# Output stage of a hybrid decoder layer: residual rows of x in the four tiles of the RWKV bonus terms instead of the ring of eleven

## The chip, the cores and the metric

The kernel runs on one core of a Trainium2 chip. A core has a matrix engine (TensorE, here PE), a vector engine (VectorE, DVE), a scalar engine (ScalarE, ACT), a general engine (GpSimd, POOL) and a sync engine (SyncE, SP); each works through its own list of instructions in order, and they wait for each other by semaphores. Tiles live in SBUF, matmul results in eight PSUM banks. Data moves by DMA, which SP and ACT issue here. The metric is the time of one execution on the device in microseconds (us), as the median of several runs.

## The reference

One layer over 2048 tokens of width 1024, in float32. Three branches read the normalised x: RWKV-7 time mixing (a), sliding-window attention with a window of 128 (b), and cross-attention into 256 memory tokens (c). Each branch is projected, weighted by a sigmoid gate and summed; one more projection and the residual end the layer.

```python
h = rms_norm(x, norm_g[l])
p = h @ w_in[l]
...
bonus = jnp.sum(rh * kh * r_k.astype(f32), axis=-1, keepdims=True) * vh
return y + bonus.reshape(bsz, t, RW_WIDTH)
...
merged = (gates[:, :, 0] * (y_a @ w_proj_a[l]) + gates[:, :, 1] * (y_b @ w_proj_b[l])
          + gates[:, :, 2] * (y_c @ w_proj_c[l]))
x = x + (merged.astype(x.dtype) @ w_out[l]).astype(x.dtype)
```

The bonus term of the second fragment and the last line are what the change touches.

## The kernel before

**Blocks and stages.** The tokens are worked in four blocks of 512 (`sb` 0 to 3). In a block come the projections with RWKV, attention and cross-attention woven together; then the gates and projections of branch a (`merge`, with gates from `gate`), which finish the eight merged sums; then `output`. Ahead of `output`, the block also prepares the next one: `rope_tables` (L554 to L587) makes the rotary tables from `positions`; `x_scales` loads the next 512 rows of x in eight pieces (L1326, on ACT's queue), squares and sums them on ACT (L1328), adds the halves on DVE (L1330), turns the sums into scales, and spreads them over a tile with a copy (L543) and transposes on PE (L545); `x_cols` loads x transposed (L1344), multiplies by the scales (L1347) and splits the result in two (L1350).

**Matmuls in three.** Every number that goes through a large matmul is split into a high part, rounded on ACT, and a remainder, on DVE; each product then takes three matmuls (high by high, high by low, low by high). For a block of weights, `wblock` loads into a tile `raw` (L486 issues on SP), splits on ACT (L487) and DVE (L488) into a tile `whl`, and, in block 0, stores `whl` to memory (L491), so that blocks 1 to 3 load it ready (L483). The projection of L505 to L507 is the general matmul of this kind. `split_y` splits a finished branch (L1032 ACT, L1033 DVE), `split_acc` the merged sums (L1289 ACT, L1291 DVE).

**The output stage** (`output`, L1294 to L1309) makes the 1024 columns in two halves `n`. A half has four PSUM banks, one for each 128 tokens, `mm`, `as_`, `mm`, `as_`, two tiles of each name, so the second half takes the same four banks as the first. Eight weight blocks follow each other, and each is multiplied into the four banks (L1301 to L1303: 8 x 4 x 3 matmuls a half). Then for each of the four banks a tile is taken, a 128x512 piece of x is loaded into it on ACT's queue (L1307), DVE adds half the bank to it in place (L1308; the merged sums carry a factor of two), which frees the bank, and the tile is written out, on ACT's queue too (L1309).

**Tiles.** Tiles of one name share a fixed number of buffers, given out in turn, first in, first out; a request waits until the buffer that is next has been let go. The row tile of `output` is a `g2`, of which there are eleven (`NG`). `g2` also holds the gates of branch a (L1269), the high parts of the merged sums (`a` in L1288, one for each of the eight k, all read until the last matmul of the second half), and other gates earlier in the block. The tiles named `ya` (pool `yp`, four buffers) hold the RWKV bonus term of each of four pairs of heads: written at L839 while the block's RWKV inputs are prepared, added to and gated at L1009 and L1010, and last read by the split of branch a (L1032, L1033), ahead of the merge. The name also serves for the first four tiles of x transposed at the start of the program.

**What sets the order.** The code is not run in the order in which it is written. A planner (`steps`, `lay_out`, `order`) takes all instructions with their dependences, models each engine's clock with a duration for each instruction, and hands every engine its list: among those that can start it takes the lowest rank, which is roughly the place in the program, with weight loads and splits up to 1000 places ahead and the reads of PSUM up to 600. An instruction that is the first to use a tile is offered only when the tile's turn has come and a buffer is free in the model. A change of tiles therefore changes the lists. The DMAs of SP and ACT take eight semaphores in turn (`DMAHW0` to `DMAHW7` below), across both queues; a DMA that comes to a semaphore waits, on the engine that issues it, until the DMA before it on that semaphore has landed.

Of the kernel before, what the change touches and what calls it, by code (L numbers as in the profile page):

```python
# [316 lines left out]
def build(tc, A, nsb=4):  # L317
# [19 lines left out]
    def g2(dt=F32, shape=(128, TB)):  # L337
        return gp_.tile(list(shape), dt, name="g2")
# [3 lines left out]
    def mm_ps():  # L342
        return ps.tile([128, 512], F32, name="mm", bufs=2)
# [4 lines left out]
    def s_ps():  # L348
        return ps.tile([128, 512], F32, name="as_", bufs=2)
# [40 lines left out]
    def yrow(name):  # L390
        return yp.tile([128, TB], F32, name=name)
# [88 lines left out]
    def wblock(src, key=None):  # L480
        w = wp.tile([128, 2, 512], F32R, name="whl")
        if key in kept:
            nc.sync.dma_start(w.bitcast(F32), kept[key])  # L483
            return w[:, 0], w[:, 1]
        raw = wp.tile([128, 512], F32, name="raw", bufs=RAW)
        nc.sync.dma_start(raw, src)  # L486
        S.activation(w[:, 0], raw, AF.Copy)  # L487
        V.tensor_tensor(w[:, 1], raw, w[:, 0].bitcast(F32), op=ALU.subtract)  # L488
        if key is not None and nsb > 1:
            kept[key] = dp.tile([128, 2, 512], F32, name=f"k{len(kept)}")  # L490
            nc.sync.dma_start(kept[key], w.bitcast(F32))  # L491
        return w[:, 0], w[:, 1]
# [801 lines left out]
    def output(sb, mh, ml):  # L1294
        for n in range(2):
            op = [mm_ps(), s_ps(), mm_ps(), s_ps()]
            for k in range(8):
                wh, wl = wblock(A["w_out"][n, k], ("out", n, k))
                for tt in range(4):
                    tk = slice(tt * 128, (tt + 1) * 128)  # L1300
                    PE.matmul(op[tt], mh[k][:, tk], wh, start=k == 0, stop=False)  # L1301
                    PE.matmul(op[tt], mh[k][:, tk], wl, start=False, stop=False)  # L1302
                    PE.matmul(op[tt], ml[k][:, tk], wh, start=False, stop=k == 7)  # L1303
            for tt in range(4):
                rows = slice(sb * TB + tt * 128, sb * TB + (tt + 1) * 128)
                xr = g2()
                nc.scalar.dma_start(xr, A["x"][rows, n * 512:(n + 1) * 512])  # L1307
                V.scalar_tensor_tensor(xr, op[tt], 0.5, xr, op0=ALU.mult, op1=ALU.add)  # L1308
                nc.scalar.dma_start(A["out"][rows, n * 512:(n + 1) * 512], xr)  # L1309
# [53 lines left out]
    for sb in range(nsb):  # L1363
# [9 lines left out]
        ya, yb, yc_ = ([], []), ([], []), ([], [])  # L1373
# [45 lines left out]
        if rb is not None:  # L1419
            hT = x_cols(sb + 1, rb)  # L1420
        output(sb, *zip(*parts))
    order(tc, manual, groups, follow)
    es.close()
# [90 lines left out]
```

## Time and profile before

| | |
|---|---|
| median of 3 timed runs | 2163.45 us (2163.43 to 2164.69) |
| the profiled execution | 2162.26 us, of which the span of the profile is 2160.5 |
| PE | 99% of the span busy, 14260 matmuls |
| DVE | 1556.2 us busy, 72% |
| ACT | 830.3 us busy, 38% |
| POOL | 131.9 us busy, 6% |
| DMA | 511.87 MB, 237 GB/s over the span |

A row of a group of instructions reads: line, engine, operation, out<-in by the names of the program with their shapes, how many; busy time, the mean of one in ns; the idle time of the engine just before them, and what ended it. A list of waits gives the engine and the waiting line, who ended the wait, and us in total, how often, and the longest. A timeline row gives the start in us, the duration, and in brackets the wait ahead of it. The table of windows gives for a stretch from A to B its length, the busy time of each of PE, DVE, ACT, POOL and SP (with the count of instructions that were alone in it in brackets), then the granted TensorE clock as a share of full speed, the busy share of the DMA engines, and GB/s.

### The profile page before, as it was taken

How to read it: one execution, taken by the hardware profiler on the slowest of the kernel's cores; microseconds unless marked ns; L12 is line 12 of the kernel's file. 1: busy time of each engine (PE TensorE's matmuls, PEld its weight loads, DVE VectorE, ACT ScalarE, POOL GpSimd, SP SyncE). 2: the span in 40 equal slices, each digit the busy share in tenths (PEclk: the TensorE clock that was granted, in tenths of full speed). 3: DMA queues.
4: the chain of work that ended last, by engine and by line, in shares of the span. 5: the costliest groups of instructions: out<-in, count | busy, mean ns of one | idle time of the engine just before them, and what ended most of it. 6: DMA issues, size and time to landing. Idle time of an engine off the chain costs nothing.

```text
span 2160.5 us, 37816 instructions
## 1 busy us (share of the span) xinstructions
PE 2132.1 (99%) x14260; PEld 1757.0 (81%) x14260; DVE 1556.2 (72%) x3731; ACT 830.3 (38%) x1757; POOL 131.9 (6%) x159
## 2 busy tenths in 40 slices
PE   8999999999999999999999999999999999999999
PEld 6888787777788888878888888887888888887887
DVE  7799999567578979754627988955455798894532
ACT  6655554336244353303414344421522434431220
POOL 2001000001000000001000100000100000000100
PEclk9999999999999999999999999999999999999999
DMA  9988787978866566585876656676676655758556
GB/s 324 333 273 266 256 280 236 345 272 307 322 231 206 181 211 203 182 293 179 279 260 208 197 185 205 207 250 212 230 259 233 208 184 194 225 173 288 184 193 204
DMA packets 254758, 511.87 MB, mean 237 GB/s; under 512 B 38256, under 2 KB 120432, under 8 KB 254576
## 3 DMA queue, kind: packets, MB, share of 16 engines
q1 hardware_dynamic: 238448, 480.08, 66.8%
q10 hardware_dynamic: 16128, 29.37, 4.1%
q8 instruction: 113, 1.85, 0.3%
q14 instruction: 69, 0.57, 0.1%
HBM read 375.67 MB, written 133.69 MB: 236 GB/s over the span
## 4 chain that ended last, share of the span: by engine, by line
PE 82%; DVE 8%; DMA 6%; issue 1%; ACT 1%; SPq 0%; POOL 0%; ACTq 0%; DVEq 0%; POOLq 0%
PE mm L507 20%; PE mm L505 20%; PE mm L506 20%; DVE whl L488 2%; DMA rt<-in_x 1%; DMA k<-whl 1%; PE mm L1303 1%; PE mm L1301 1%; PE mm L1302 1%; PE rw L983 1%; PE rw L966 1%; PE oo L1250 1%; PE rw L806 1%; DVE ibc L863 1%; PE rw L826 1%
## 5 line engine op out<-in xcount | busy, mean ns | idle before, releaser
L505 PE MATMUL mm<-hH,whl 128*128 128x512 f32 x1888 | 746.0, 395 | 2.9 <-DVE carry L714 2.8
L506 PE MATMUL mm<-hL,whl 128*128 128x512 f32 x1888 | 743.5, 394 | 1.5 <-DVE hL L1350 1.4
L507 PE MATMUL mm<-hH,whl 128*128 128x512 f32 x1888 | 744.6, 394 | 0.0
L505 PEld LDWEIGHTS mm<-hH,whl 128*128 128x128 f32 x1888 | 355.1, 188 | 74.4 <-ACT g L1018 3.2
L506 PEld LDWEIGHTS mm<-hL,whl 128*128 128x128 f32 x1888 | 355.4, 188 | 72.2 <-DVE hL L1350 2.5
L507 PEld LDWEIGHTS mm<-hH,whl 128*128 128x128 f32 x1888 | 355.3, 188 | 70.9
L487 ACT ACTIVATE whl<-raw 128x512 fp32r<-128x512 f32 x162 | 101.6, 629 | 155.7 <-PE mm L507 105.2
L505 PE MATMUL mm<-yh,whl 128*128 128x512 f32 x384 | 151.0, 394 | 2.8 <-ACT ibc L1328 1.6
L507 PE MATMUL mm<-yh,whl 128*128 128x512 f32 x384 | 151.9, 395 | 0.0
L506 PE MATMUL mm<-yl,whl 128*128 128x512 f32 x384 | 150.7, 392 | 0.0
L488 DVE TENSOR_TENSOR whl<-raw,whl 128x512 fp32r<-128x512 f32 x162 | 111.6, 690 | 41.6 <-ACT whl L487 39.7
L863 DVE STREAM_SHUFFLE ibc<-Nc 128x496 f32<-128x496 f32 (+30 forms) x248 | 114.2, 472 | 0.0
L1269 ACT ACTIVATE gt<-mm 128x512 f32<-128x512 f32 x64 | 38.0, 594 | 190.0 <-PE mm L507 189.8
L864 DVE TENSOR_TENSOR ibc<-ibc,Yi 128x496 f32<-128x496 f32 (+30 forms) x248 | 104.5, 421 | 4.2
L865 DVE TENSOR_TENSOR Yi<-Yi,ibc 128x496 f32<-128x496 f32 (+30 forms) x248 | 103.3, 417 | 1.0
L505 PEld LDWEIGHTS mm<-yh,whl 128*128 128x128 f32 x384 | 72.1, 188 | 18.5 <-ACT ibc L1328 2.0
L506 PEld LDWEIGHTS mm<-yl,whl 128*128 128x128 f32 x384 | 72.2, 188 | 15.3 <-DVE yl L1033 0.4
L507 PEld LDWEIGHTS mm<-yh,whl 128*128 128x128 f32 x384 | 72.1, 188 | 15.3
L463 POOL TENSOR_SCALAR st<-st 128x4 f32<-128x4 f32 (+1 forms) x32 | 13.1, 409 | 1031.5 <-DVE st L1060 468.9
L1308 DVE SCALAR_TENSOR_TENSOR g<-mm,g 128x512 f32<-128x512 f32 x16 | 11.0, 690 | 88.5 <-PE mm L1303 88.5
L1284 DVE SCALAR_TENSOR_TENSOR gt<-gt,mm 128x512 f32<-128x512 f32 x32 | 22.0, 686 | 68.5 <-PE mm L507 68.1
L1218 ACT ACTIVATE g<-g,mxs,st 128x128 f32<-128x128 f32 x128 | 61.5, 484 | 18.7 <-DVE mxs L1211 18.7
(1836 smaller groups left out, 3678.5 us busy)
## 6 DMA issues: line engine op xcount, KB each, us to landing
whl<-k SPq DMA_DIRECT2D x486, 512.0 KB, 3.5
k<-whl SPq DMA_DIRECT2D x162, 512.0 KB, 4.7
raw<-in_w_in SPq DMA_DIRECT2D x118, 256.0 KB, 3.7
fq<-big SPq DMA_DIRECT2D x64, 256.0 KB, 4.3
fb<-big SPq DMA_DIRECT2D x64, 256.0 KB, 4.6
big<-fq SPq DMA_DIRECT2D x32, 512.0 KB, 6.7
big<-fb SPq DMA_DIRECT2D x32, 512.0 KB, 5.8
g<-in_x ACTq DMA_DIRECT2D x32, 256.0 KB, 4.8
```

The costliest lines, as they stand in the source:

```text
L487: S.activation(w[:, 0], raw, AF.Copy)
L488: V.tensor_tensor(w[:, 1], raw, w[:, 0].bitcast(F32), op=ALU.subtract)
L505: PE.matmul(out, lh, rh, start=i == 0, stop=False)
L506: PE.matmul(out, lh, rl, start=False, stop=False)
L507: PE.matmul(out, ll, rh, start=False, stop=i == n - 1)
L806: m = PE.matmul(g[:, c], BK[h, c0 + c], Q[h, c0 + c], start=True, stop=True)
L863: V.stream_shuffle(bc[:, :, :w], N_[:, :, s + 1:], [s] * 32)
L864: V.tensor_tensor(bc[:, :, :w], bc[:, :, :w], Y[:, :, s:s + 1].to_broadcast([128, n, w]), op=ALU.mult)
L865: V.tensor_tensor(Y[:, :, s + 1:], Y[:, :, s + 1:], bc[:, :, :w], op=ALU.add)
L1218: S.activation(P_, P_, AF.Exp, scale=r2[:, b, i:i + 1], bias=mx[:, b, i:i + 1], accum_out=mx[:, b, 2 + i:3 + i])
L1269: S.activation(t, gp, AF.Tanh, scale=0.5)
L1284: V.scalar_tensor_tensor(g, g, 1.0, pp, op0=ALU.add, op1=ALU.mult)
```

## The change

One line of `output` asks for another tile. `yrow("ya")` gives the next of the four `ya` tiles, where `g2()` gave the next of eleven.

```diff
             for tt in range(4):
                 rows = slice(sb * TB + tt * 128, sb * TB + (tt + 1) * 128)
-                xr = g2()
+                xr = yrow("ya")
                 nc.scalar.dma_start(xr, A["x"][rows, n * 512:(n + 1) * 512])
                 V.scalar_tensor_tensor(xr, op[tt], 0.5, xr, op0=ALU.mult, op1=ALU.add)
                 nc.scalar.dma_start(A["out"][rows, n * 512:(n + 1) * 512], xr)
```

Each block asks for eight `ya` tiles more, after the four of its bonus terms: the first half's four rows take over from the bonus terms, the second half's four from the first half's rows, and the next block's bonus terms from the second half's rows. The planner makes new lists from this. Numbers behind a tile's name below count tiles through the program; tiles of one number are the same one.

PE, block 1, the start of the output stage's second half. `mm_11684`, `as__11685`, `mm_11686` and `as__11687` are the four banks, `whl_11688` is the first weight block; rows with + are new in the place, rows with - gone from it. First, behind the first weight block's matmuls into the third bank:

```order
 L1302 MATMUL mm_11686<-whl_11688,g2_11359 128x512
 L1303 MATMUL mm_11686<-whl_11688,mB_11361 128x512
+L1301 MATMUL as__11687<-whl_11688,g2_11359 128x512
+L1302 MATMUL as__11687<-whl_11688,g2_11359 128x512
+L1303 MATMUL as__11687<-whl_11688,mB_11361 128x512
 L1301 MATMUL mm_11684<-whl_11702,g2_11380 128x512
 L1302 MATMUL mm_11684<-whl_11702,g2_11380 128x512
```

And behind the third weight block's matmuls into the third bank:

```order
 L1302 MATMUL mm_11686<-whl_11716,g2_11401 128x512
 L1303 MATMUL mm_11686<-whl_11716,mB_11403 128x512
-L1301 MATMUL mm_11684<-whl_11730,g2_11422 128x512
-L1302 MATMUL mm_11684<-whl_11730,g2_11422 128x512
-L1301 MATMUL as__11687<-whl_11688,g2_11359 128x512
-L1302 MATMUL as__11687<-whl_11688,g2_11359 128x512
-L1303 MATMUL as__11687<-whl_11688,mB_11361 128x512
-L1301 MATMUL as__11687<-whl_11702,g2_11380 128x512
-L1302 MATMUL as__11687<-whl_11702,g2_11380 128x512
-L1303 MATMUL as__11687<-whl_11702,mB_11382 128x512
 L1301 MATMUL as__11687<-whl_11716,g2_11401 128x512
 L1302 MATMUL as__11687<-whl_11716,g2_11401 128x512
```

Before, the first two weight blocks were multiplied into the fourth bank only after the third weight block had been through the other banks; now each block goes through all four in turn. It is the same in the second halves of blocks 0, 2 and 3. PE's list differs otherwise only in a few rows ahead of block 0's output.

ACT, block 0, in the merge of branch a, around the split of the fourth branch tile (`yh_5921<-ya_3628`). The names in brackets are the semaphores that an instruction waits for. Before:

```order
L1032 ACTIVATE yh_5921<-ya_3628 128x512 [waits DVE_49]
L487 ACTIVATE whl_6049<-raw_6050 128x512 [waits DMAHW2_49,DMAHW5_49,PE_49,Activation_49]
L487 ACTIVATE whl_6075<-raw_6076 128x512 [waits DMAHW5_49,DMAHW7_49,PE_49,Activation_49]
L1269 ACTIVATE g2_5866<-mm_5827 128x512
L1326 DMA rt_5952<-in_x 128x512 [waits Activation_49]
L1326 DMA rt_5956<-in_x 128x512 [waits DMAHW6_49,DMAHW4_49,DVE_49]
L1326 DMA rt_5960<-in_x 128x512 [waits DMAHW7_49,DVE_49]
L487 ACTIVATE whl_6101<-raw_6102 128x512 [waits DMAHW1_49,PE_49]
```

After:

```order
L1032 ACTIVATE yh_5921<-ya_3628 128x512 [waits DVE_49]
L1307 DMA ya_6415<-in_x 128x512 [waits DMAHW3_49,DVE_49]
L487 ACTIVATE whl_6049<-raw_6050 128x512 [waits DMAHW4_49,PE_49]
L487 ACTIVATE whl_6075<-raw_6076 128x512 [waits DMAHW0_49,PE_49]
L1269 ACTIVATE g2_5866<-mm_5827 128x512
L1326 DMA rt_5952<-in_x 128x512
L1326 DMA rt_5956<-in_x 128x512 [waits DMAHW7_49,DMAHW2_49]
L1326 DMA rt_5960<-in_x 128x512 [waits DMAHW3_49,DVE_49]
L487 ACTIVATE whl_6101<-raw_6102 128x512 [waits PE_49]
L1326 DMA rt_5964<-in_x 128x512 [waits DMAHW4_49,DVE_49]
```

The load of the first half's fourth row (`ya_6415`) now follows the split that last reads its tile on ACT, and waits for the same split on DVE (L1033); the other three stand in the same way behind the splits of the other three tiles. The third load of the next block's x (`rt_5960`) waits for `DMAHW3`, which is the semaphore that the load of `ya_6415` takes. On DVE the L1033 of this tile has moved up by one place, to the one straight behind the cast of the positions (L568).

ACT, block 0, further on, where the last squares for the next block's scales (L1328) and the copies of the merged sums (L1289) stand. Before:

```order
L1326 DMA rt_5980<-in_x 128x512 [waits DMAHW4_49,Activation_49]
L487 ACTIVATE whl_6251<-raw_6252 128x512 [waits DMAHW3_49,PE_49]
L1289 ACTIVATE g2_6019<-mB_2375 128x512
L1289 ACTIVATE g2_6045<-mB_2483 128x512 [waits DVE_49]
L1328 ACTIVATE ibc_5970,ss_5951<-rt_5968 128x512 [waits DMAHW7_49]
L1328 ACTIVATE ibc_5974,ss_5951<-rt_5972 128x512 [waits DMAHW0_49]
L487 ACTIVATE whl_6270<-raw_6271 128x512 [waits DMAHW5_49,PE_49]
L1328 ACTIVATE ibc_5978,ss_5951<-rt_5976 128x512 [waits DMAHW2_49,Activation_49]
L1289 ACTIVATE g2_6071<-mB_2845 128x512 [waits DVE_49]
L1328 ACTIVATE ibc_5982,ss_5951<-rt_5980 128x512 [waits DMAHW4_49,Activation_49]
L487 ACTIVATE whl_6289<-raw_6290 128x512 [waits DMAHW1_49,PE_49]
L1289 ACTIVATE g2_6097<-mB_3017 128x512 [waits DVE_49]
```

After:

```order
L1326 DMA rt_5972<-in_x 128x512
L487 ACTIVATE whl_6251<-raw_6252 128x512 [waits DMAHW6_49,DMAHW0_49,PE_49]
L1326 DMA rt_5976<-in_x 128x512
L1326 DMA rt_5980<-in_x 128x512
L1289 ACTIVATE g2_6019<-mB_2375 128x512
L1289 ACTIVATE g2_6045<-mB_2483 128x512 [waits DVE_49]
L1289 ACTIVATE g2_6071<-mB_2845 128x512 [waits DVE_49]
L487 ACTIVATE whl_6270<-raw_6271 128x512 [waits DMAHW2_49,DMAHW1_49,PE_49]
L1328 ACTIVATE ibc_5974,ss_5951<-rt_5972 128x512 [waits DMAHW5_49,Activation_49]
L1328 ACTIVATE ibc_5978,ss_5951<-rt_5976 128x512 [waits DMAHW7_49,Activation_49]
L487 ACTIVATE whl_6289<-raw_6290 128x512 [waits DMAHW6_49,DMAHW4_49,PE_49]
L1328 ACTIVATE ibc_5982,ss_5951<-rt_5980 128x512 [waits DMAHW0_49,Activation_49]
```

Before, two copies stood ahead of the last four squares, and the third behind the seventh square; now three copies stand ahead of the last three squares, with the last three loads ahead of them. The fifth load (`rt_5968`) and its square stand further up now: the load ten rows ahead of this piece, ahead of the table load of L583, where before it stood behind L585.

In all four blocks the loads L1307 of the first half that stood between the copies L1289 and the first writes L1309 are gone from that place. In block 3 ACT's list there now has the four writes of the first half, then the four loads of the second half; before, the fourth load of the first half and two of the second stood behind the third write, and the other two behind the fourth. On DVE the four adds L1308 of a half stand together now; in block 0 a weight split (L488) stood ahead of the fourth. The place of the last weight splits ahead of block 0's first L1308 is unchanged. SP's list differs in one place, two weight stores at the end of block 0, and POOL's not at all.

## The prediction

> **What bounds the kernel now.** I read the page's busy shares first, then the list of what TensorE (PE) waited for, then the timeline around each output stage.
>
> ```profile
> PE 2132.1 (99%) x14260; PEld 1757.0 (81%) x14260; DVE 1556.2 (72%) x3731; ACT 830.3 (38%) x1757; POOL 131.9 (6%) x159
> ```
>
> PE is busy for 99% of a 2160.5 us span, so the only time to be won is in the few places where it stops. The list of PE's waits from 450 us on, before the first output stage, to the end names them (engine, line, what ended the wait: us in total, times, longest).
>
> ```profile
> PE mm L1301 <- DVE g L1308: 2.9, 1, 2.9
> PE mm L505 <- ACT ibc L1328: 1.6, 1, 1.6
> PE as__5988 L545 <- DVE rt L543: 1.4, 1, 1.4
> PE as__22023 L1301 <- DVE g L1308: 1.3, 1, 1.3
> PE as__16912 L1301 <- DVE g L1308: 0.9, 1, 0.9
> PE as__11333 L545 <- DVE rt L543: 0.6, 1, 0.6
> PE as__11687 L1301 <- DVE g L1308: 0.2, 1, 0.2
> ```
>
> Four rows end with L1308, the residual add that frees a PSUM bank: one in each output stage, between its two halves. The others (L1328, L543) lie just ahead of an output stage, where x is loaded and scaled for the next block: 1.6 and 1.4 us in block 0, 0.6 in block 1. The chain of work that ended last shows what is behind the wait in block 3 (start, us, what).
>
> ```profile
> 2131.45 0.70 DVE g L1308
> 2132.17 2.71 DMA out<-g
> 2134.95 5.42 DMA g<-in_x
> 2140.57 0.70 DVE g L1308
> 2141.31 0.50 PE as__22023 L1301
> ```
>
> ```profile
> 2132.81 0.69 DVE L1308 SCALAR_TENSOR_TENSOR g<-mm,g 128x512 f32<-128x512 f32 x1
> ...
> 2154.81 0.69 DVE L1308 SCALAR_TENSOR_TENSOR g<-mm,g 128x512 f32<-128x512 f32 x1 [13.55 <-PE mm L1303]
> ```
>
> The fourth row of x is not loaded until the first half's first row has been written out and its ring tile is free. In DVE's timeline the third add starts at 2132.81, so the fourth comes 7.1 us behind its end; the last row is the second half's first add. PE has already put the fourth bank's matmuls off, and still stops for it. In block 0 the picture differs:
>
> ```profile
> 547.02 3.52 ACTq L1307 DMA_DIRECT2D g<-in_x  x3
> 552.38 0.63 ACT L487 ACTIVATE whl<-raw 128x512 fp32r<-128x512 f32 x1 [5.26 <-DMA g<-in_x]
> L488 DVE TENSOR_TENSOR whl<-raw,whl x3: 684/684/686, 561.2 to 565.2; 128x512 fp32r<-128x512 f32 x3
> 565.76 0.68 DVE L1308 SCALAR_TENSOR_TENSOR g<-mm,g 128x512 f32<-128x512 f32 x1
> 566.60 0.55 PE L1301 MATMUL mm<-whl,g 128*128 128x512 f32 x1 [2.87 <-DVE g L1308]
> ...
> 570.32 0.40 PE L1301 MATMUL mm<-whl,g 128*128 128x512 f32 x1
> 570.55 0.39 PE L1302 MATMUL mm<-whl,g 128*128 128x512 f32 x1
> ```
>
> ACT's queue holds three row loads at 547, and the weight split behind them (L487) comes 5.26 us late. VectorE (DVE), which does the other half of these splits (L488), has three of them left between 561.2 and 565.2, reaches the first L1308 only at 565.76, and PE stops for 2.87 us. After the stop nine matmuls take 570.32 - 566.60 = 3.72 us, against 9 x 0.23 = 2.07 at the later spacing: **1.65 us more**, in the window of the first row below, whose granted clock (third number from the end) is 0.68.
>
> ```profile
> 565.00:570.00 5.00, 3.40 (x9) 2.68 (x10) 3.34 (x6) 0.63 (x1) 0.00 (x0) 0.68 1.00 337
> 262.00:270.00 8.00, 5.16 (x21) 0.79 0.89 287
> ```
>
> The second row holds the other long stop, 8.00 - 5.16 = 2.84 us, and its clock is below 1 too. In the window of the two stops of 1.6 and 1.4 us, further down, it is 1.00.
>
> **The change, part by part.** No instruction is added or removed. The 32 row loads (L1307) get other tiles; with them move the first half's loads on ACT's queue, and then the planner's order of PE, DVE and ACT.
>
> *Blocks 1 to 3, between the halves.* All four rows now stand loaded before the first half ends, since the four tiles are free once the last split has read them. The fourth L1308 follows the third directly, at 2132.81 + 0.69 = 2133.5, and ends at 2134.2. PE now takes the fourth bank in turn. The stop ended at 2141.31, after 1.3 us of idling and 29 matmuls of 0.23 us; so the half began near 2133.3, and its tenth matmul is due near 2135.4, 1.2 us after the bank is free. The three stops go: 1.3 + 0.9 + 0.2 = **2.4 us**. Next to be late there is nothing on PE; the second half's rows now wait for the first half's writes:
>
> ```profile
> 588.97 2.38 ACTq L1309 DMA_DIRECT2D out<-g  x4
> 647.77 0.69 DVE L839 TENSOR_TENSOR ya<-rw,gt 128x512 f32<-128x512 f32 x1
> L1307 ACTq DMA_DIRECT2D g<-in_x x32: 334/335/610, 547.0 to 2143.4; - x32
> ...
> DMA to landing us min/median/max: 2.6/4.8/7.2
> ```
>
> In block 3 the fourth write starts at 2134.2 and takes 2.7 us by the chain's row; with the slowest landing of an L1307 (last row above: 7.2) the fourth row is in by 2144.1, 10 us before the second half's first add at 2154.8. ACT has nothing else queued there. Gone, that cover would cost what lands past 2154.8. The next block's bonus terms (L839) must now wait for the last writes: issued by 591.4, first needed at 647.8. The eleven-tile ring gets eight requests fewer a block, and nothing on PE waits for it: 0.
>
> *Block 0, between the halves.* The three loads at 547 are gone from ACT's queue, with the 5.26 us in front of L487. DVE's order still puts the last L488 before the first L1308. The last three splits start between 561.2 and 565.2 now, with steps of the next block's scaling between them; with some 4 us of the delay gone DVE should come to L1308 near 562, before PE ends the half at 563.7. I take the whole stop and its slow stretch: 2.87 + 1.65 = **4.52 us**. The other bound is 0, if DVE stays as late as it is.
>
> *The first half's loads, in their new place.* Each holds ACT's queue 0.335 us (the L1307 row) and waits for DVE's second half of a split (L1033). In blocks 1 to 3 the row behind it on ACT waits for PE anyway: 0. In block 0 the first three cost nothing either. The fourth is another matter:
>
> ```profile
> 508.52 0.43 DVE L568 CAST rt<-rt 128x512 f32<-128x512 int32 x1 [1.18 <-DMA rt<-in_positions]
> 509.39 0.68 DVE L1033 TENSOR_TENSOR yl<-ya,yh 128x512 fp32r<-128x512 f32 x1
> 511.41 0.86 ACTq L1326 DMA_DIRECT2D rt<-in_x  x2
> ```
>
> Its L1033 now stands straight behind the cast of the positions: issue near 508.52 + 0.43 + 0.68 = 509.6, landing (median 4.8) near 514.4. The third of the next block's loads (L1326, issued at about 511.9 now) waits for the same semaphore, so it slips 2.5 us, and behind it on ACT wait weight splits, the squares L1328, and the other five loads. What ends there is this chain:
>
> ```profile
> 510.00:515.00 5.00, 5.00 (x24) 4.15 (x23) 4.86 (x10) 1.75 (x3) 0.00 (x0) 1.00 0.70 167
> 530.00:540.00 10.00, 6.96 (x32) 1.00 0.90 322
> 534.13 0.47 PE L505 MATMUL mm<-yh,whl 128*128 128x512 f32 x1 [1.64 <-ACT ibc L1328]
> 524.92 8.30 DMA rt<-in_x
> 542.48 9.45 DMA rt<-in_xt
> 535.18 0.16 DVE rs L1330
> 537.66 0.83 DVE rt L543
> 538.54 0.66 PE L545 MATMUL as__5988<-c_ident,rt 128*128 128x128 f32 x4 [1.40 <-DVE rt L543]
> DMA to landing us min/median/max: 3.1/4.7/8.3
> ```
>
> The last load lands at 533.22, and PE's transposes start 5.3 us later. In the new order the fifth load stands ahead of the table load and the last three behind its square; I put the last one's issue at 526 to 528 and, by the L1326 landings (last row: 4.7 to 8.3), its landing at 530.7 to 536.3, middle 533.5: no shift of the transposes. But the copies L1289, which stood behind a square and so gave PE the 1.64 us stop, now stand ahead, so PE arrives 1.64 us sooner and its loss becomes **one stop of 3.04 us**. Both stops of 2.8 us and more shown above have a clock below 1 behind them, these two short ones have 1.00: I take + **1.65 us**. Bounds: all of it gone, -3.04; landing at 536.3, +3.1 + 1.65 = +4.7.
>
> The page "TensorE: Matmul & The Clock Gate" of the Trainium skill says, in "HAM oscillation — how this bites in real kernels", that idle gaps above some 3.4 us lower the clock. The two stops of 2.84 and 2.87 us with slow matmuls behind them speak against so long a gap being needed. By that figure neither slow stretch would count as the stop's price: -4.52 would be -2.87 and +1.65 would be 0, the same sum.
>
> **Sum:** -2.4 - 4.52 + 1.65 = **-5.27 us**. The profiled execution took 2162.26 us (span 2160.5 and 1.8 around it), so 2157.0 for one like it; the median of the three timed runs is 2163.45, 1.2 above, and I forecast **2158.2** against that. About 0.2%, 4.3 us, is what a measurement of this kernel can tell from no change.
>
> **Rivals.** (1) *The chain before block 0's output gets shorter.* For it: the weight split that stood ahead of L1330 on DVE no longer waits behind the last square on ACT, and no row loads crowd the queues at 547. Against: the later third load. With half of the 3.04 us gone and no slow stretch: -6.9 - 1.5 = -8.4, 2155.0. (2) *Block 0's stop stays.* The last L488 still stands ahead of L1308 and needs its weight load; ACT and DVE hand work to each other in turn, and that, not the loads at 547, may set when the last split is done. Then -2.4 + 1.65 = -0.75, 2162.7. (3) *The change doesn't do what it says:* with four tiles, the second half's rows queue for the first half's writes and PE stops for them instead. That needs landings 7 us later than the slowest; 2163.5. (4) *Slower.* Three landings in block 0 now follow each other on ACT: the fourth row, the fifth L1326, the last L1326. My middle gave them 4.8, 4.7 and 6.5: 16.0 us. At 9.45 each, the longest load of that fence, it is 28.35, so PE stops 12.35 us longer: -6.92 + 1.65 + 12.35 = +7.1, 2170.5. Slower than before begins at 5.3 us more, three landings of 7.1. Against it: in the window of the first row of that fence, where the first of the three falls, DMA is busy 0.70, not full.
>
> The page "DMA: Bandwidth & Descriptors" of the Trainium skill, "Anatomy of one DMA — SWDGE (gpsimd) path", states that DMA engines never wait for semaphores, the issuing sequencer does. That is rival 4's ground, and the 5.26 us before L487 agree.
>
> **How the numbers follow.** Forecast 0.50, rival 1 0.24, rival 2 0.17, rival 3 0.03, rival 4 0.06 (0.05 of it past 4.3 us). Faster than 2159.1 are rival 1 and most of the forecast: 0.68. Within 0.2%: the rest of it, rivals 2 and 3: 0.27. Slower: 0.05. The range, 2154.0 to 2162.8, goes from rival 1 with 2.5 of its 3.04 us to rival 2; it leaves out rivals 3 and 4 and what lies beyond those two.
>
> **What would show it.** Right: no PE wait on L1308 in any output stage, four L1308 rows in one piece, no load of x on ACT's queue at 547. One PE stop of about 3 us at the L545 transposes before block 0's output, with a granted clock below 1 behind it. Wrong: PE still waiting near 564, PE waits elsewhere (L505 on L1269 or on whl), or in blocks 1 to 3 an L1308 that waits for a DMA.

## The result, and the profile after

| | before | after |
|---|---|---|
| median of 15 timed runs | 2162.48 us (2159.72 to 2166.57) | 2157.64 us (2153.32 to 2161.03) |
| the profiled execution | 2162.26 us, span 2160.5 | 2155.11 us, span 2153.3 |

The ratio of after to before is 0.9976, with a 95% interval of 0.9968 to 0.9985: 5.2 us faster, 3.2 to 6.9. The forecast was 2158.2, inside its range of 2154.0 to 2162.8. The total came out as forecast; block 0's part of it did not, as the experiments show.

The list of PE's waits in the changed kernel from 450 us on, as it was shown for before (engine, line, what ended the wait: us in total, times, longest):

```profile
PE as__5988 L545 <- DVE rt L543: 3.8, 1, 3.8
PE mm L505 <- ACT g L1269: 0.4, 1, 0.4
PE rw L1002 <- DVE rt L999: 0.3, 1, 0.3
```

No row ends with L1308: all four stops between the halves are gone. What remains is one long stop at the transposes ahead of block 0's output, 3.8 us in place of the two of 1.6 and 1.4. In block 3 DVE's timeline after (start, us, what, wait ahead of it in brackets) shows why there is no stop:

```profile
2126.57 0.69 DVE L1308 SCALAR_TENSOR_TENSOR ya<-as__21889,ya 128x512 f32<-128x512 f32 x1
2127.25 0.69 DVE L1308 SCALAR_TENSOR_TENSOR ya<-mm,ya 128x512 f32<-128x512 f32 x1
2127.93 0.69 DVE L1308 SCALAR_TENSOR_TENSOR ya<-as__21891,ya 128x512 f32<-128x512 f32 x1
2147.65 0.69 DVE L1308 SCALAR_TENSOR_TENSOR ya<-mm,ya 128x512 f32<-128x512 f32 x1 [19.03 <-PE mm L1303]
```

The fourth add follows straight behind the third, where 7.1 us lay between them. The last row is the second half's first add: it waits for PE alone, though its row of x came in late, behind the first half's write, as ACT's timeline shows:

```profile
2126.62 2.38 ACTq L1309 DMA_DIRECT2D out<-ya  x4
2129.44 5.51 ACTq L1307 DMA_DIRECT2D ya<-in_x  x4
```

Ahead of block 0's output, PE's timeline and a window of the same place (length, then busy time of PE, PEld, DVE, ACT and POOL, granted clock, DMA share, GB/s):

```profile
537.73 1.12 PE L545 MATMUL as__5988<-c_ident,rt 128*128 128x128 f32 x4 [3.75 <-DVE rt L543]
538.50 0.78 PE L506 MATMUL mm<-yl,whl 128*128 128x512 f32 x1
...
540.68 0.39 PE L505 MATMUL mm<-yh,whl 128*128 128x512 f32 x1
538.50:541.00 2.50, 2.50 (x9) 2.04 (x8) 2.24 (x4) 1.75 (x3) 0.00 (x0) 0.59 0.70 205
```

Five matmuls take 540.68 - 538.50 = 2.18 us, 1.0 more than at 0.23 each, and the four transposes 0.46 more than before's 0.66: some 1.5 us of slow matmuls stand behind the stop.

**A measure by stretches.** PE is busy nearly all the time, so a loss in a block shows as the time between two landmarks of equal work. I take the start of the fourth gate of branch a in block 0 (up to it PE's lists are the same, but for four transposes that stand one matmul further down), the first gate of block 1, and the end of the span. The landmarks in ACT's timeline before:

```profile
496.03 0.58 ACT L1269 ACTIVATE g<-mm 128x512 f32<-128x512 f32 x1
728.83 0.60 ACT L1269 ACTIVATE gt<-mm 128x512 f32<-128x512 f32 x1 [1.70 <-PE mm L507]
```

And after:

```profile
493.36 0.60 ACT L1269 ACTIVATE g<-mm 128x512 f32<-128x512 f32 x1
725.02 0.60 ACT L1269 ACTIVATE gt<-mm 128x512 f32<-128x512 f32 x1 [1.69 <-PE mm L507]
```

The first landmark is not quite even. The fourth gate stands behind other work in ACT's two lists, and the last matmul that it reads starts 0.44 us ahead of it before (first row) and 0.14 us after (second row):

```profile
495.59 0.39 PE L507 MATMUL mm<-hH,whl 128*128 128x512 f32 x1
493.22 0.39 PE L507 MATMUL mm<-hH,whl 128*128 128x512 f32 x1
```

By PE's rows, block 0's stretch is therefore 0.3 us shorter, against before's, in every kernel with the new order in block 0 than the figures below say. The second landmark has no such difference (0.43 and 0.42 us).

From block 1's first gate to the end it is 2160.48 - 728.83 = 1431.65 us before and 2153.33 - 725.02 = 1428.31 after: 3.3 us less, the forecast 2.4 and a little more. Block 0's stretch is 232.80 before and 231.66 after: 1.1 us less (1.4 by PE's rows), where 2.9 were forecast. The remaining 2.7 us (2.4 by PE's rows) lie ahead of the fourth gate, where PE does the same work in the same order: that much two executions differ by themselves. So a single pair of profiles can't settle a term of 2 us, and the experiments repeat them.

### The profile page after: what moved, and what is told of

It is laid out like the page before. It is cut to its first block, busy times and chain, and to the rows that moved or that the text cites. A ratio compares the mean times of both kernels' runs of the same rounds, so it can differ in the third digit from the quotient of the medians.

```text
span 2153.3 us, 37785 instructions
## 1 busy us (share of the span) xinstructions
PE 2131.2 (99%) x14260; PEld 1755.6 (82%) x14260; DVE 1557.1 (72%) x3731; ACT 830.0 (39%) x1757; POOL 131.3 (6%) x159
## 4 chain that ended last, share of the span: by engine, by line
PE 85%; DVE 8%; DMA 3%; issue 1%; ACT 1%; POOL 0%; SPq 0%; ACTq 0%; DVEq 0%; POOLq 0%
PE mm L507 21%; PE mm L505 21%; PE mm L506 21%; DVE whl L488 2%; PE mm L1301 1%; PE mm L1303 1%; PE mm L1302 1%; PE rw L983 1%; PE rw L966 1%; DMA k<-whl 1%; DVE ibc L863 1%; PE oo L1250 1%; PE rw L806 1%; DVE Yi L865 1%; PE rw L826 1%
## 5 line engine op out<-in xcount | busy, mean ns | idle before, releaser
L505 PE MATMUL mm<-hH,whl 128*128 128x512 f32 x1888 | 745.3, 395 | 2.9 <-DVE carry L714 2.8
L505 PEld LDWEIGHTS mm<-hH,whl 128*128 128x128 f32 x1888 | 355.1, 188 | 74.4 <-ACT g L1018 3.2
L487 ACT ACTIVATE whl<-raw 128x512 fp32r<-128x512 f32 x162 | 101.5, 628 | 149.3 <-PE mm L507 104.0
L505 PE MATMUL mm<-yh,whl 128*128 128x512 f32 x384 | 151.2, 394 | 1.6 <-ACT gt L1269 1.2
L488 DVE TENSOR_TENSOR whl<-raw,whl 128x512 fp32r<-128x512 f32 x162 | 111.7, 690 | 42.0 <-ACT whl L487 40.0
L1308 DVE SCALAR_TENSOR_TENSOR ya<-mm,ya 128x512 f32<-128x512 f32 x16 | 11.0, 690 | 107.4 <-PE mm L1303 107.4
L505 PEld LDWEIGHTS mm<-yh,whl 128*128 128x128 f32 x384 | 72.3, 188 | 18.2 <-ACT gt L1269 1.6
L1284 DVE SCALAR_TENSOR_TENSOR gt<-gt,mm 128x512 f32<-128x512 f32 x32 | 22.0, 687 | 68.1 <-PE mm L507 67.7
```

The source lines that it names most:

```text
L505: PE.matmul(out, lh, rh, start=i == 0, stop=False)
L1284: V.scalar_tensor_tensor(g, g, 1.0, pp, op0=ALU.add, op1=ALU.mult)
```

## Experiments

Each run below was timed against executions of the kernel before on its own chip. The chips differ between rows (the kernel before had medians of 2159.5 to 2162.5 us on them), so compare the ratios and not the medians. The table has one row for each; "block 0" and "blocks 1 to 3" are the two stretches of its one profile, and the last columns the PE stops in block 0 at L545 and at L1301 for L1308.

| kernel | median us | ratio (95%) | block 0 | blocks 1 to 3 | L545 | L1301, block 0 |
|---|---|---|---|---|---|---|
| before (profile above) | 2162.48 | | 232.80 | 1431.65 | 1.4 (and 1.6 at L505) | 2.9 |
| before, again | 2162.37 | 0.9996 (0.9987 to 1.0005) | 230.99 | 1432.49 | 3.1 | none for L1308 |
| after (profile above) | 2157.64 | 0.9976 (0.9968 to 0.9985) | 231.66 | 1428.31 | 3.8 | none |
| after, again | 2158.71 | 0.9981 (0.9972 to 0.9990) | 232.21 | 1428.92 | 4.2 | none for L1308 |
| ya in blocks 1 to 3 | 2155.91 | 0.9980 (0.9970 to 0.9989) | 230.94 | 1428.93 | 3.0 | 1.3 |
| the same, again | 2156.57 | 0.9983 (0.9974 to 0.9992) | 230.03 | 1427.94 | 2.5 | 0.9 |
| ya in block 0 | 2161.00 | 1.0003 (0.9994 to 1.0013) | 232.37 | 1431.02 | 4.4 | none |
| the same, again | 2162.96 | 1.0012 (1.0003 to 1.0020) | 233.26 | 1432.15 | 4.4 | 1.3 |
| ya for the fourth row | 2154.74 | 0.9972 (0.9963 to 0.9980) | 230.40 | 1428.35 | 2.5 | 0.5 (second bank) |
| after, row four moved | 2157.57 | 0.9987 (0.9978 to 0.9995) | 232.34 | 1429.12 | 4.0 | none |
| after, load five moved | 2156.02 | 0.9970 (0.9959 to 0.9980) | 229.49 | 1429.11 | 2.0 | none |
| after, scales first | 2151.01 | 0.9945 (0.9933 to 0.9958) | 228.22 | 1428.23 | 1.4 | none |
| before, scales first | 2164.96 | 1.0022 (1.0012 to 1.0033) | 232.73 | 1438.14 | 0.8 | 3.4 |

### Which blocks gain

```diff
-                xr = yrow("ya")
+                xr = yrow("ya") if sb else g2()      # blocks 1 to 3
+                xr = g2() if sb else yrow("ya")      # block 0
```

The two kernels split the change cleanly: the lists of each part are those of before or of the changed kernel.

> Only blocks 1 to 3 take the ya tiles; block 0 keeps the ring of eleven, and its lists are those of before. Theory (the gain in blocks 1 to 3 is the three stops of PE on L1308 between the halves, 1.3, 0.9 and 0.2 us): PE waits for L1308 in block 0 alone (2.9 us, with a granted clock below 1 behind it), the two stops ahead of block 0's output stay at 1.6 and 1.4 us, and the time is 2.4 us below before, 2160.1 against a median of 2162.5. Rival (the stops go, but the work behind them is bound by something else, so that the time comes back in the next block): no L1308 wait in blocks 1 to 3 and no change of the time, 2162.5.

> Only block 0 takes the ya tiles; blocks 1 to 3 keep the ring, and block 0's lists are those of the changed kernel. Theory (block 0 gains its stop of 2.87 us and 1.65 us of slow matmuls between the halves, and pays for the longer stop ahead of its output, 3.75 us with some 1.5 us of slow matmuls where 1.64 and 1.40 us stood): one PE stop of 3.8 us at L545, no L1308 wait in block 0, the waits of 1.3, 0.9 and 0.2 us in blocks 1 to 3 as before, and the time 2.3 us below before, 2160.2. Rival (the stop ahead of the output gives back all that the other one brings): within 0.5 us of before.

With the tiles in blocks 1 to 3 alone, PE's waits from 450 us on are

```profile
PE as__5988 L545 <- DVE rt L543: 3.0, 1, 3.0
PE mm L1301 <- DVE g L1308: 1.3, 1, 1.3
PE as__16558 L545 <- DVE rt L543: 0.7, 1, 0.7
PE as__11333 L545 <- DVE rt L543: 0.3, 1, 0.3
```

and with the tiles in block 0 alone

```profile
PE as__5988 L545 <- DVE rt L543: 4.4, 1, 4.4
PE as__16912 L1301 <- DVE g L1308: 1.2, 1, 1.2
PE as__22023 L1301 <- DVE g L1308: 0.8, 1, 0.8
PE as__11687 L1301 <- DVE g L1308: 0.3, 1, 0.3
...
```

The stops between the halves of blocks 1 to 3 are there without the tiles and gone with them. But block 0 of the first kernel, which runs the lists of before, shows one stop of 3.0 us and then 1.3, not 1.6, 1.4 and 2.9. And block 0 alone brings nothing: the theory's -2.3 us fell, its rival stood. Both were run again, with before and after:

> The ya tiles in blocks 1 to 3 alone, once more. From block 1's first gate (L1269) to the end of the span the three profiles with the lists of before took 1431.0 to 1432.5 us, those with the ya tiles 1428.3 to 1429.1. If that is all that the tiles bring there, the stretch is 1428 to 1429.3 again, and the ratio of the timed runs 0.9987 (the first time 0.9980, interval 0.9970 to 0.9989); block 0 is that of before, 230.9 to 232.8.

> The ya tiles in block 0 alone, once more. If they bring nothing there, the ratio of the timed runs is 1.000 again (1.0003 the first time, interval 0.9994 to 1.0013), with block 0's stretch at 231.7 to 232.4 and a stop of 3.7 to 4.4 us at L545; if the prediction's 2.9 us are there on most runs, 0.9987.

> The kernel before once more, unchanged, for a second profile of its blocks 1 to 3 and a third of block 0's lists (the run with ya tiles in blocks 1 to 3 alone had the second). From the fourth gate of branch a in block 0 (L1269) to the first gate of block 1 the first profile took 232.80 us, the run with ya tiles in blocks 1 to 3, with the same lists there, 230.94. If the PE stop of 2.87 us at L1301 with its 1.65 us of slow matmuls is what block 0's lists give every time, this stretch is 232.5 to 233 and the stop 2.9; if it was one draw of several, the stretch is 231 and the stop 1 to 2 us, without slow matmuls. In blocks 1 to 3 the waits for L1308 are 0.2, 0.9 and 1.3 us, within 0.3. The time is that of before: ratio 1.000.

> The changed kernel once more, unchanged. The same stretch of block 0 took 231.66 us in its profile, and 232.37 in the run that has the ya tiles in block 0 alone. If the change gains nothing in block 0, the stretch is 231.5 to 232.5, with one stop of 3.7 to 4.4 us at L545; if it gains the 2.9 us that the prediction had, 230. The time is 4 to 6 us below before (ratio 0.9972 to 0.9981).

The table gives the means of four profiles each. From block 1 on, the ring of eleven takes 1431.8 us, the ya tiles 1428.5: **-3.3 us**, with no overlap of the two groups (1431.0 to 1432.5 against 1427.9 to 1428.9). In block 0 the lists of before take 231.2 (230.0 to 232.8), those of the change 232.4 (231.7 to 233.3): **+1.2 us**, or +0.9 by PE's rows, with an overlap. The timed runs say the same of the signs: block 0 alone gives ratios of 1.0003 and 1.0012, the second with an interval above 1.

### One tile is enough

```diff
-                xr = yrow("ya")
+                xr = yrow("ya") if tt == 3 else g2()
```

> Only the fourth row of each half takes a ya tile, the other three stay with the ring of eleven. Theory (in blocks 1 to 3 the ring is one tile short: eight of its eleven tiles hold the high parts of the merged sums until the last matmul, so three are left for four rows): one tile is enough there, no L1308 wait in blocks 1 to 3, -2.4 us. In block 0 the three row loads stay on ACT's queue ahead of the second half's splits, two of them apart from the third. If it is these loads that make the splits late, PE still stops at the half in block 0, 1 to 2.9 us, and the time is 2160 or a little below; the rival there (the fourth row alone made PE stop) has no stop in block 0 and 2155.5. The load of the first half's fourth row now comes ahead of the third split of branch a, where it does not meet the loads of the next block's x, so the theory has the two stops ahead of block 0's output at 1.4 to 3.1 us together, without slow matmuls.

Blocks 1 to 3 take 1428.35 us, as with all rows in ya tiles: the ring was one tile short. In block 0 the row loads stayed on ACT's queue and PE stopped between the halves for 0.5 us: less than the one answer had and more than the other. The time, a ratio of 0.9972 or some 6 us, is nearer to the second answer's (7.0 us below 2162.5) than to the first's (2.5). The stop at L545 is 2.5 us, within the expected 1.4 to 3.1, but slow matmuls followed it, which were not expected.

### What makes the stop ahead of block 0's output longer

The prediction laid it on the fourth row's load, for whose semaphore the third load of the next block's x waits. One instruction was moved:

```diff
+                    x_scales.last = nc.scalar.dma_start(xr, ...)          # L1326
...
+                d = nc.scalar.dma_start(xr, ...); sb == n == 0 and tt == 3 and behind(d, x_scales.last)
```

> The changed kernel with one instruction moved: in block 0 the load of the first half's fourth row is put behind the last load of the next block's x on ACT; every other list is the same. Theory (that load holds the third load of x back, which waits for its semaphore, and so moves the whole chain of scales by some 2.2 us): the last load of x lands 1.5 to 2.5 us sooner against PE's work, the stop of 3.75 us at L545 falls to 1.3 to 2.3 us, no matmuls run slowly behind it, and the time is 3 to 4 us below the changed kernel, 2154. Rival (the last landings are set by the traffic and by the squares that free their tiles, not by that load): the stop stays within 0.5 us of 3.75, and the time that of the changed kernel, 2157.6.

The third load now goes out directly behind the second, but the later ones don't gain by it (ACT's queue with that load moved):

```profile
509.93 0.82 ACTq L1326 DMA_DIRECT2D rt<-in_x  x2
510.85 0.60 ACTq L1326 DMA_DIRECT2D rt<-in_x  x1
515.26 0.33 ACTq L1326 DMA_DIRECT2D rt<-in_x  x1
518.49 0.34 ACTq L1326 DMA_DIRECT2D rt<-in_x  x1
524.15 0.36 ACTq L1326 DMA_DIRECT2D rt<-in_x  x1
524.95 1.02 ACTq L1326 DMA_DIRECT2D rt<-in_x  x2
```

The stop stays at 4.0 us and the block at 232.3: the theory fell. In this list and in the changed kernel's, the fifth load (518.49 here) stands ahead of the table load and of squares two to four, which free the tiles for loads six to eight. By its list it waits there for its semaphore, and the table load waits behind it. In the changed kernel's ACT timeline it goes out at 518.87, 0.9 us after ACT was done with the first square:

```profile
517.26 0.62 ACT L1328 ACTIVATE ibc<-rt 128x512 bf16<-128x512 f32 x1
517.78 0.19 ACT L1328 ACTIVATION_READ_ACCUMULATOR ibc<-rt 128x1 f32 x1
518.87 0.34 ACTq L1326 DMA_DIRECT2D rt<-in_x  x1
519.24 1.28 ACT L583 ACT_TABLE_LOAD   x1 [1.26 <-DMA raw<-in_w_proj]
...
525.16 0.47 ACTq L1326 DMA_DIRECT2D rt<-in_x  x1
```

The last load is issued 525.16 - 493.36 = 31.8 us behind the fourth gate; before, 524.92 (its row stands in the prediction) - 496.03 = 28.9. So the fifth load alone was put back behind L585:

```diff
+            rope_tables.last = S.activation(nf, an, AF.Sin, scale=0.5)    # L585
...
+                    d = nc.scalar.dma_start(xr, ...); (sb, i, u) == (1, 2, 0) and behind(d, rope_tables.last)
```

> The changed kernel, with the fifth load of the next block's x in block 0 put behind L585, where before has it; the planner then also puts the second square back ahead of the table load. The early load of the fourth row stays. Theory (in the new order ACT waits at the fifth load until its semaphore is free, at 518.1 to 518.8, and the squares behind it, which free the tiles of loads six to eight, come late): loads six to eight are issued 1 to 2 us sooner against PE's work, the stop at L545 falls from 3.8 to 4.4 us to 1.5 to 3 us, and the stretch from block 0's fourth gate of branch a to block 1's first gate is 230 us in place of 231.7 to 232.4; the time is 1.5 to 2.5 us below the changed kernel. Rival (the loads' landings of 6 to 9 us under the weight traffic set it): the last load lands as late, the stop stays at 3.5 or more, the time is the changed kernel's.

```profile
522.99 0.34 ACTq L1326 DMA_DIRECT2D rt<-in_x  x1
PE as__5988 L545 <- DVE rt L543: 2.0, 1, 2.0
```

The last load (first row) goes out 522.99 - 492.58 = 30.4 us behind this run's fourth gate, 1.4 us sooner. The stop halves, and the block takes 229.5 us, 2.2 less than the lowest of the changed kernel's. By this one profile the theory stands: the place of the fifth load, and of the second square that moved with it, made the chain late, not the row load. The timed ratio of 0.9970 points the same way, but its interval overlaps with those of the changed kernel.

### The chain taken out of the way

```diff
-            rope_tables(sb + 1)
             rb = x_scales(sb + 1)
+            rope_tables(sb + 1)
```

> The changed kernel, with the next block's scales written ahead of its rotary tables in every block, so that all eight loads of x stand ahead of the table load on ACT and the last square 10 places ahead of it. If the chain from the loads of x to the transposes L545 is what PE stops for ahead of block 0's output, the stop of 3.8 to 4.4 us and the slow matmuls behind it go, and the stretch of block 0 is 227 to 228.5 us, the time 3.5 to 5 us below the changed kernel, 2153. If the tables, now late, become the next thing PE stops for, the waits name L583 or L587's tables in block 1, and the time is that of the changed kernel or above.

> The kernel before (ring of eleven for all rows), with the next block's scales written ahead of its rotary tables, as in the run that did so with the ya tiles. Theory (in block 0 PE loses its time to one chain, the loads and squares of the next block's x, which shows now as a stop at L545, now as one between the halves; the ya tiles move it and bring nothing there; in blocks 1 to 3 they bring 2.9 us): with the chain early, both stops of block 0 are below 1.5 us without the ya tiles too, the stretch from block 0's fourth gate of branch a to block 1's first gate is 228 to 229 us, the waits for L1308 in blocks 1 to 3 stay at 1.5 to 2.5 us together, and the time is 3 to 4 us above that run, 2154 to 2155. Rival (the row loads on ACT's queue ahead of block 0's output hold the splits, whatever the scales do): PE waits 1.3 to 2.9 us for L1308 in block 0 and the stretch is 230 to 231.

With the ya tiles PE's waits from 450 us on shrink to

```profile
PE as__5962 L545 <- DVE rt L543: 1.4, 1, 1.4
PE mm L505 <- ACT g L1269: 0.9, 1, 0.9
PE rw L1002 <- DVE rt L999: 0.3, 1, 0.3
```

and the time is 2151.01 us, 11.9 below before by the ratio: the best of all kernels here. With the ring of eleven the same edit makes the kernel slower than before, and my theory of it fell: in its profile the stops between the halves grew.

```profile
PE mm L1301 <- DVE g L1308: 3.4, 1, 3.4
PE as__16912 L1301 <- DVE g L1308: 2.5, 1, 2.5
PE as__11687 L1301 <- DVE g L1308: 1.9, 1, 1.9
PE as__22023 L1301 <- DVE g L1308: 1.1, 1, 1.1
```

ACT's and DVE's timelines of that kernel show the mechanism in block 0:

```profile
557.74 3.07 ACTq L1344 DMA_DIRECT2D rt<-in_xt  x2
560.85 2.97 ACTq L1307 DMA_DIRECT2D g<-in_x  x2
563.87 0.63 ACT L487 ACTIVATE whl<-raw 128x512 fp32r<-128x512 f32 x1 [5.70 <-DMA rt<-in_xt]
...
564.53 0.69 DVE L488 TENSOR_TENSOR whl<-raw,whl 128x512 fp32r<-128x512 f32 x1 [3.24 <-ACT whl L487]
565.14 0.68 DVE L1308 SCALAR_TENSOR_TENSOR g<-mm,g 128x512 f32<-128x512 f32 x1
```

Two loads of x transposed and two row loads hold ACT's queue for 6 us; the split L487 behind them comes 5.70 us late, so does L488, and the first add behind that. The kernel with the ya tiles has the two loads of x transposed there too, but no row loads, and its split comes some 3 us sooner behind the fourth gate. The tiles are worth 4.5 us in block 0 here (232.73 against 228.22), and 9.9 in blocks 1 to 3. In blocks 1 to 3, 5.5 of this are the three stops, and two of them had slow matmuls too: the granted clock is 0.94 from 1080 to 1110 us and from 1610 to 1640. Of the ring's kernel this is one profile, of an execution 3.1 us above its median (2168.06 against 2164.96).

## Why the prediction was right in sum and wrong in a part

**Blocks 1 to 3: right, a little too small.** The three stops went and the fourth add follows the third, as worked out. Forecast -2.4 us, measured -3.3 by the stretches. The timed runs of that part alone say more, 0.9980 and 0.9983, 4.3 and 3.7 us, both with 3.3 inside their intervals.

**The second half's rows behind the first half's writes: right.** They cost nothing; the adds wait for PE. The next block's bonus terms (L839) make nobody wait either.

**Block 0, between the halves: the step that failed.** The prediction took "the whole stop and its slow stretch: 2.87 + 1.65 = 4.52 us" from one profile as what block 0 always loses there. The same lists gave stops of 2.9, 1.3, 0.9 and none in four executions; where it was none, 3.1 us had been lost at L545 already, with a granted clock of 0.50 behind it, and the block took 231.0 us against 232.8. (The lists of the change, too, gave one of 1.3 us once.) The window of that run, the second of before:

```profile
535.00:540.00 5.00, 3.98 (x12) 3.30 (x13) 4.90 (x9) 1.94 (x4) 0.68 (x1) 0.50 0.92 300
```

Nor did the stop go for the reason that the prediction gave. It had DVE reach the first add near 562, 66.0 us behind the fourth gate, once the row loads are gone from ACT's queue. In the changed kernel they are gone, and ACT and DVE show

```profile
561.96 0.63 ACT L487 ACTIVATE whl<-raw 128x512 fp32r<-128x512 f32 x1 [0.74 <-PE as__6250 L1303]
563.24 0.68 DVE L1308 SCALAR_TENSOR_TENSOR ya<-mm,ya 128x512 f32<-128x512 f32 x1
```

The add starts 563.24 - 493.36 = 69.9 us behind the gate, no sooner than before's 565.76 - 496.03 = 69.7. The last split ahead of it now waits for PE. And PE, held up longer at L545, comes to the second half at 564.48, 71.1 us behind the gate, where it was due at 563.7, 67.7 behind it, before. So the stop is gone from the changed kernel because PE comes some 3 us later, not because the add comes sooner.

Row loads can hold the splits, as the prediction had it: with the chain ahead taken away, the lists with them stop for 3.4 us and those without them do not. Where they stand matters: with the fourth row alone in a `ya` tile, three row loads are still on the queue, two of them apart from the third, and the first add comes 563.08 - 495.38 = 67.7 us behind the gate, as early as without them and with load five moved (560.33 - 492.58 = 67.8). But in the kernel as it is, PE comes late from L545, and by then most of that delay is over. The change removes a delay that another one mostly hides.

**Block 0, ahead of the output: right in kind, wrong in cause, too small.** One stop with slow matmuls behind it was forecast at 3.04 us, and it was 3.8 to 4.4; the slow matmuls cost some 1.5 us, near the 1.65 forecast. The prediction's mechanism, "the third of the next block's loads ... waits for the same semaphore, so it slips 2.5 us", was not what counts: freed of it, the stop stayed. The prediction names the fifth load's new place but gives it no cost; it makes ACT wait and holds back the squares that free the tiles of the last three loads. The time that it gave for the last load's issue, 526 to 528, came out all the same: 525.16, in a profile that is 2.4 us ahead of before's by PE's rows. But the load took 8.5 us to land (525.16 to 533.65), where the middle of the forecast had 6.5.

Together block 0 was forecast at -4.52 + 1.65 = -2.9 and gave +1.2, or +0.9 by PE's rows (four profiles each, with overlap). What stays open: the stretches add up to -3.3 + 1.2 = -2.1 us (-2.4 by PE's rows), while the whole change was timed at -5.2 and -4.1, with intervals of -6.9 to -3.2 and -6.1 to -2.2. The ratios of the parts multiply to 0.9983 and 0.9995, against 0.9976 and 0.9981. Each of these is known to about 0.0009, and a profile is one execution; the missing 2 to 3 us were not found in any one place. So it is in part luck that the total met the forecast: it was not made of the parts that the forecast was worked out from.

## What to carry to other kernels

A ring that is one tile short shows as a transfer that waits for another transfer; give that one request a tile that is free at that time (here the fourth row alone was enough) before moving all of them. Where a planner or any list order follows from tile counts, look at what else has moved: the cost and its repair lay in loads that the edit did not touch. And a stop seen in one profile is one draw: where two delays lie in series, the first hides the second, so profile twice before pricing the second, and take the first away first: with the scales written ahead, the same tiles brought 0.0077 of the time (1.0022 against 0.9945), some three times as much.

## What the runs showed of the hardware

Shorter stops than those of the prediction were followed by slow matmuls. Behind the stop of 2.02 us at L545 in the kernel with load five moved, the granted clock was 0.66 over 5 us, with PE busy throughout:

```profile
535.00:540.00 5.00, 5.00 (x17) 4.07 (x18) 4.21 (x8) 1.76 (x4) 0.00 (x0) 0.66 0.87 274
```

Behind the stop of 1.4 us in the kernel with the ya tiles and the scales first it was 1.00:

```profile
522.00:528.00 6.00, 5.41 (x26) 4.56 (x27) 5.30 (x9) 2.19 (x4) 0.25 (x1) 1.00 0.91 294
```

The page "TensorE: Matmul & The Clock Gate" of the Trainium skill puts the gap that lowers the clock above some 3.4 us ("HAM oscillation — how this bites in real kernels"); the 2.02 us here speak against it.

The length of a stop does not settle it either. The stop of 2.84 us that the prediction showed near 264 us, with a clock of 0.79 over its window, is in all 13 profiles at 2.83 to 2.86 us, and in five of them no slow matmuls follow. With the ya tiles in blocks 1 to 3, the same window reads

```profile
262.00:270.00 8.00, 5.17 (x33) 4.25 (x32) 7.11 (x15) 3.63 (x7) 0.00 (x0) 1.00 0.89 294
```

The first 25 matmuls behind that stop take 4.3 us in those five profiles, 5.7 to 5.9 in seven and 7.1 in one. One and the same stop thus brings no slow matmuls, 1.5 us of them or 2.8 us, from one execution to the next.

The times go with the granted clock: of the changed kernel's 15 runs, the seven with a mean granted clock of 0.997 took 2157.1 us on average, the three at 0.995 2159.9, the one at 0.999 2153.3.
